# A quarter of the K and Q products of groups two to four computed as seven products of 2x2 blocks

## The chip, the cores and the metric

The kernel runs on one NeuronCore of one Trainium2 chip. TensorE multiplies matrices into PSUM; VectorE and ScalarE work on SBUF and PSUM; GpSimd does little here; SyncE issues nearly all DMA transfers. The engines run at the same time, each through its own queue in order, and wait for each other by semaphores. The metric is the device time of one execution, in microseconds.

## The reference

A decoder layer for 256 tokens of width 2048, in float32. Cut to what this change touches:

```python
h = rmsnorm(x, norm_mix_w[l])
proj = jnp.einsum('bsd,de->bse', h, w_in[l])
q, k, v, z, b_raw, a_raw, p_in, g_a, g_b = jnp.split(proj, splits, axis=-1)
qkv = jax.nn.silu(causal_dwconv(jnp.concatenate([q, k, v], axis=-1), conv_qkv_w[l]))
q, k, v = jnp.split(qkv, 3, axis=-1)
...
o = gated_delta_rule(q, k, v, g_log, beta).astype(x.dtype)
o = rmsnorm(o, gdn_norm_w[l]) * jax.nn.silu(z.reshape(bsz, seq, N_HEADS, HEAD_DIM))
...
mixed = jax.nn.sigmoid(g_a) * y_a + jax.nn.sigmoid(g_b) * y_b
x = x + jnp.einsum('bsd,de->bse', mixed, w_out[l])
```

Q, K, V, Z, the pooled input and the gates g_a and g_b are each 256 x 2048 products of the normalised tokens with a 2048 x 2048 part of `w_in`. The delta rule works in chunks of 64 tokens and solves a lower triangular system per chunk and head. Behind this come the output projection and a gated MLP with an up and a down projection.

## The kernel before

**Groups and weight tiles.** The 2048 output columns of each projection are cut into four groups of 512 (four heads each). A group computes K, Q, V, the pooled input, the gate GB, Z, a small pool product and the gate GA, in this order (the last group has the pool product and Z the other way round), and then the next group starts with K. Each projection of a group reads the 2048 features as eight weight tiles of 256 features (two feature blocks of 128) by 512 columns, 512 KB in float32. The names GA0 to GA7, K0 to K7 and so on below are these tiles.

**High and low parts.** TensorE multiplies in a float32 form of reduced precision, so each weight tile is cut in two: ScalarE casts `raw` to `whi` (L317), VectorE computes `wlo` = `raw` - `whi` (L328, "the split"). The tokens were cut the same way, into `xh` and `xl`. `gemm_a` multiplies per feature block and half of the tokens `whi` with `xh`, `whi` with `xl` and `wlo` with `xh` (L365 to L367): 12 matmuls of 512 columns a tile. The sums of a projection stand in a PSUM tile of pool `psm`, two banks, one per half of the tokens, and `psm` has two such tiles; `psg` has four of one bank.

**What sets the order.** The list `srcs` gives the weight tiles in their order of use. Whenever a product takes a tile from `weights`, tiles up to two further ahead are begun (`begin`: cast and split), and their loads (`load`) go into SyncE's queue; `raw` has four buffers, `whi` and `wlo` three. Between feature blocks `side()` advances a generator of side work, here the gated delta rule of the group (`gdn`); `later` holds functions that run when the next product has come to its second tile (`if c == 1`). The tile scheduler then orders each engine's queue by its own simulation of time; each engine works its queue strictly in order.

**The delta rule at a group's end.** While GA runs, the group's triangular systems are solved. VectorE does a forward substitution on small blocks (`tb`, L965 and L967). The result goes to DRAM and back (`tbd`, L972 and L975) and is transposed block by block on VectorE into `T` (L987). Then the inverse is put together from the blocks: TensorE L1011 (with L1018 beside it, from which VectorE makes `ro`, L1022), ScalarE copies into `U` (L1014), TensorE L1029, VectorE L1031 and L1032 (into `T` and `TT`), TensorE L1039, a ScalarE copy (L1041), TensorE L1047, VectorE L1048, and then the products with V and Q. At the same time the gate of Z stands in `sz`; after GA it is multiplied by GA's gate (ScalarE L1177, VectorE L1204) and by a norm weight (L1206).

**The up stage** of the MLP has for some of its column chunks another form already: the 2x2 blocks of a pair of weight chunks are loaded as four `quad` tiles, and seven products stand in for eight (the Winograd form of Strassen's scheme), named T1, 11, T2, 21, T3, 22 and T4. The products T1 to T4 take differences of blocks (`up_sum`, L244 on VectorE, in place), and T1, T2, T3 and 22 take sums of tokens. Between the products sums are copied or added in PSUM (ScalarE L1447 and L1451, VectorE L1433 and L1454). `high_first` issues one such product: six matmuls of 512 columns, the four with `whi` first.

Of the kernel before, what the change touches and what calls it, by code (L numbers as in the profile page):

```python
# [14 lines left out]
P = 128  # L15
S = 256
# [19 lines left out]
def kernel(  # L36
# [40 lines left out]
    def cols(w, base, nk):  # L77
        return [w[c * 256 : (c + 1) * 256, base : base + 512].rearrange("(k p) f -> p k f", p=P)
                for c in range(nk // 2)]

    srcs = []
    for g in range(4):
        for base in (C_K, C_Q, C_V, C_P, C_GB):
            srcs += cols(w_in[0], base + 512 * g, KD)
# [6 lines left out]
        srcs += cols(w_in[0], C_GA + 512 * g, KD)  # L91
# [6 lines left out]
    UP_PARTS = ("T1", "11", "T2", "21", "T3", "22", "T4")  # L98
    up_w = [(cols(w_up[0], 512 * c, KD), cols(w_up[0], DFF + 512 * c, KD)) for c in range(NUP)]
    up_steps = []  # L100
    TAIL = 3
    for c in range(NUP):
# [114 lines left out]
    def load_part(n, k):  # L217
        if n == len(loads):
            if isinstance(srcs[n], tuple):
# [9 lines left out]
    UP_HOMES = ((("xt0", "xt1", "xt2", "xt3"), ("hhi8", "hlo8", "hhi9", "hlo9")),  # L229
                (("xt0", "xt2", "xt1", "xt3"), ("hhi6", "hlo6", "hhi7", "hlo7")))  # L230

    def quad_load(c, n):

        ch, i = n // 4, (1, 0, 3, 2)[n % 4]
        up_quarters[c, ch, i] = fp.tile([P, 2, 512], F32, tag=UP_HOMES[1 - c % 2][ch][i], name=nm("quad"))
# [58 lines left out]
    def begin(n):  # L294
        while len(made) < min(len(srcs), n):
            load(len(made) + 1)
            raw = loads[len(made)]
            if isinstance(raw, tuple):
                raw, plus, minus = raw
                nc.vector.tensor_tensor(raw, plus, minus, op=ALU.subtract)  # L300
            src = srcs[len(made)]
            shape = list(raw.shape)
            keep = kept.get(len(made))
            behind_conv = ExitStack()
            for ins in last_conv.values():
# [11 lines left out]
            last_cast[0] = nc.scalar.copy(hi, raw).ins  # L317
            if shape[1] == 8:
                lo = None
                nc.vector.tensor_tensor(hi[:, :, 32:64], raw[:, :, 0:32], hi[:, :, 0:32].bitcast(F32),  # L320
                                        op=ALU.subtract)
            else:
                if fourth:
                    lo = fp.tile(shape, F32R, tag="s", name=nm("wlo"))
                else:
                    lo = wpool.tile(shape, F32R, tag="wlo", name=nm("wlo")) if keep is None else \
                        mtile(4 + keep, shape, F32R, nm("klo"))
                last_split[0] = nc.vector.tensor_tensor(lo, raw, hi.bitcast(F32), op=ALU.subtract).ins  # L328
# [22 lines left out]

    later = []

    def gemm_a(lh, ll, nk, steps=None, ps=None):

        ps = pm() if ps is None else ps
        for c in range(nk // 2) if steps is None else steps:
            if c == 1:
                while later:
                    later.pop(0)()  # L360
            hi, lo = weights()
            for kk in range(2):
                k = 2 * c + kk
                for t in range(2):
                    mm(ps[:, t, :], lh(k, t), hi[:, kk, :], start=(k == 0), stop=False)  # L365
                    mm(ps[:, t, :], ll(k, t), hi[:, kk, :], start=False, stop=False)  # L366
                    mm(ps[:, t, :], lh(k, t), lo[:, kk, :], start=False, stop=(k == nk - 1))  # L367
                side()
        return ps

    banks = [0]

# [487 lines left out]
    def gdn(g, kq, vt, conv, res):  # L860
# [231 lines left out]
        yield  # L1092
        res.append((po, ro))

    for g in range(4):
        kq = mp.tile([P, 4, 2, S], F32, tag="kq", bufs=1, name=nm("kq"))
        for kind, dst in ((1, kq[:, :, 0, :]), (0, kq[:, :, 1, :])):
            ps = ps_k0 if kind == 1 and g == 0 else gemm_a(xh, xl, KD)
            e = evict(ps)
            convs.append(conv_silu(e, kind, g, dst))  # L1100
            if g:
                later.append(lambda conv=convs[-1]: sum(1 for _ in conv))
            elif kind:

                later.append(lambda conv=convs[-1]: side_work.__setitem__(0, chain(conv, running_sums())))
            else:
                later.append(drain)
# [5 lines left out]
            0, along(gdn(g, kq, vt, v_conv(g, vt), res), conv)))  # L1113
        v_taps(g)
        if g == 0:
            def after_k(k_conv=k_conv[0]):
                with tc.issue_after(last_pow[0]), tc.issue_after(k_conv):
                    fixed_parts()
# [85 lines left out]
        nc.vector.scalar_tensor_tensor(sz, ta, 1.0, sz, op0=ALU.add, op1=ALU.mult)  # L1204
        sz4 = sz.rearrange("p t (h d) -> p (t h) d", h=4)
# [104 lines left out]
    def four_sums(a11, a12, a21, a22, hi, lo):  # L1310

        s = fp.tile([P, 4, S], F32, tag="s", name=nm("sums"))
        s1, s2, s3, s4 = (s[:, n].rearrange("p (k s) -> p k s", k=2) for n in range(4))
        nc.vector.tensor_tensor(s1, a21, a22, op=ALU.add)
        nc.vector.tensor_tensor(s2, s1, a11, op=ALU.subtract)
        nc.vector.tensor_tensor(s3, a11, a21, op=ALU.subtract)
        nc.vector.tensor_tensor(s4, a12, s2, op=ALU.subtract)
# [4 lines left out]
    def by_halves(h):  # L1322
        return [h[:, 2 * j : 2 * j + 2, t * P : (t + 1) * P] for t in range(2) for j in range(2)]

    y_d = {c: dpool.tile([P, 4, S], F32, tag=f"y{c}", bufs=1, name=f"y{c}") for c in (7, 8, 9)}

# [81 lines left out]

    def fl(k, t):
        return both(fhl, k)[:, 1, t * P : (t + 1) * P]  # L1410

    def high_first(uses, w, first=False):

        for n in range(2):
            for kk in range(2):
                for ps, high, low in uses:
                    for lhs in (high, low) if n == 0 else (high,):
                        mm(ps, lhs(kk), w[n][:, kk], start=(first and n == 0 and kk == 0 and lhs is high), stop=False,  # L1418
                           skip_group_check=True)

    def up_product(c, what, ch):

# [315 lines left out]
```

## Time and profile before

| what | value |
| --- | --- |
| runs | 1537.75, 1536.89, 1536.61 us; median 1536.89 |
| profiled execution: span | 1536.8 us (the page gives no time of its own beside it) |
| instructions | 20233 |
| ScalarE busy | 853.1 us (56%) |
| GpSimd busy | 80.9 us (5%) |
| HBM traffic | 203 GB/s over the span |
| end of the last chain | PE 30% of the span, all others below 1% |

The profile is that of one execution. A row of a group of instructions has the line of the kernel, the engine, the operation, the output and inputs by their tile names, the count, and behind the bar the busy time and the mean in ns of one, then the idle time of the engine just before these instructions with what ended most of it. A row of the timeline starts with the time in us from the span's start and the duration; a number in brackets is the time for which the engine stood idle before it, with the engine, tile and line that ended the wait. A row of waits names the waiting group, the one that releases it, then the total in us, the number of waits and the longest. A row of one tile has the durations in ns (least, median, most) and the first and last start. A row of windows has the stretch, then its length, the busy us of TensorE, its weight load, VectorE, ScalarE and GpSimd, the granted TensorE clock, the DMA share and GB/s. Matmuls overlap: each lasts some 0.39 us, but they follow each other at a shorter spacing.

### The profile page before, as it was taken

What the parts mean: (1) busy time and instruction counts of PE and PEld (TensorE: products, weight loads), DVE (VectorE), ACT (ScalarE), POOL (GpSimd) and SP (SyncE); (2) the same over time, 40 slices, a digit from 0 to 9 for tenths busy, and PEclk for the clock granted to TensorE, in tenths of its full rate; (3) what the DMA queues carried; (4) which work ended last, traced back from release to release, by engine and by line L of the source; (5) the groups of instructions that cost most, each with busy time, mean ns of one, the idle gap of its engine ahead of it and who ended that gap; (6) DMA issues with size and microseconds to landing.
All of it is one profiled execution on the core that took longest, in us unless ns stands there. A gap on an engine that the chain in (4) does not pass through costs nothing. (4 is left out here: it accounts for less than half of the span.)

```text
span 1536.8 us, 20233 instructions
## 1 busy us (share of the span) xinstructions
PE 1524.3 (99%) x7290; PEld 1255.4 (82%) x7290; DVE 1268.3 (83%) x1793; ACT 853.1 (56%) x1070; POOL 80.9 (5%) x105
## 2 busy tenths in 40 slices
PE   9999999999999999999999999999999999999997
PEld 8887888787878888788888888788888888888876
DVE  6788859896589858887567899999999886889896
ACT  6455446454455445454455666666666665555553
POOL 1010002000100000000000000000000011010200
PEclk9999999999999999999999999999999999999999
DMA  8776757776576766776588556656457478566662
GB/s 276 209 229 198 203 165 207 218 216 185 148 250 201 208 169 194 231 195 186 171 263 305 179 178 219 219 206 206 154 165 243 127 238 266 172 223 207 235 201 98
DMA packets 166515, 313.62 MB, mean 204 GB/s; under 512 B 19554, under 2 KB 23426, under 8 KB 166286
## 3 DMA queue, kind: packets, MB, share of 16 engines
q1 hardware_dynamic: 157280, 283.17, 59.2%
q0 software_dynamic: 7344, 27.27, 5.5%
q10 hardware_dynamic: 1790, 1.89, 0.4%
q8 instruction: 57, 0.93, 0.3%
q14 instruction: 44, 0.36, 0.1%
HBM read 303.33 MB, written 8.95 MB: 203 GB/s over the span
## 5 line engine op out<-in xcount | busy, mean ns | idle before, releaser
L317 ACT CAST whi<-raw 128x1024 fp32r<-128x1024 f32 x420 | 441.2, 1052 | 427.1 <-PE psm L366 270.0
L328 DVE TENSOR_TENSOR wlo<-raw,whi 128x1024 fp32r<-128x1024 f32 x418 | 507.7, 1220 | 146.0 <-ACT whi L317 140.2
L317 ACT CAST whi<-quad 128x1024 fp32r<-128x1024 f32 x182 | 190.5, 1053 | 136.8 <-PE psg L1418 43.5
L328 DVE TENSOR_TENSOR wlo<-quad,whi 128x1024 fp32r<-128x1024 f32 x182 | 220.0, 1219 | 30.0 <-ACT whi L317 29.4
L367 PE MATMUL psm<-wlo,xhl 128*128 128x512 f32 x432 | 169.5, 393 | 1.3 <-DVE wlo L328 1.2
L365 PE MATMUL psm<-whi,xhl 128*128 128x512 f32 x432 | 169.0, 391 | 0.0
L366 PE MATMUL psm<-whi,xhl 128*128 128x512 f32 x432 | 168.6, 390 | 0.0
L1418 PE MATMUL psg<-whi,fhl 128*128 128x512 f32 x504 | 127.2, 390 | 0.0
L1418 PEld LDWEIGHTS psg<-whi,fhl 128*128 128x128 f32 x504 | 94.5, 188 | 19.6
L367 PEld LDWEIGHTS psm<-wlo,xhl 128*128 128x128 f32 x432 | 81.1, 188 | 18.8 <-DVE wlo L328 2.2
L366 PEld LDWEIGHTS psm<-whi,xhl 128*128 128x128 f32 x432 | 81.1, 188 | 16.8
L365 PEld LDWEIGHTS psm<-whi,xhl 128*128 128x128 f32 x432 | 81.1, 188 | 16.7
L244 DVE TENSOR_TENSOR quad<-quad,quad 128x1024 f32<-128x1024 f32 x72 | 87.6, 1216 | 0.0
L1418 PE MATMUL psg<-wlo,fhl 128*128 128x512 f32 x252 | 69.9, 389 | 0.0
L1418 PE MATMUL psg<-whi,ups 128*128 128x512 f32 x216 | 58.9, 394 | 0.0
L1418 PEld LDWEIGHTS psg<-wlo,fhl 128*128 128x128 f32 x252 | 47.3, 188 | 9.9
L1403 PE MATMUL psm<-whi,hhi 128*128 128x512 f32 (+1 forms) x140 | 54.5, 389 | 0.1
L1403 PE MATMUL psm<-whi,hlo 128*128 128x512 f32 (+1 forms) x140 | 54.1, 386 | 0.0
L1403 PE MATMUL psm<-wlo,hhi 128*128 128x512 f32 (+1 forms) x140 | 54.0, 387 | 0.0
L365 PE MATMUL psm<-whi,mhi 128*128 128x512 f32 x128 | 50.8, 397 | 0.0
L367 PE MATMUL psm<-wlo,mhi 128*128 128x512 f32 x128 | 50.0, 390 | 0.0
L366 PE MATMUL psm<-whi,mlo 128*128 128x512 f32 x128 | 49.9, 390 | 0.0
(435 smaller groups left out, 2953.7 us busy)
## 6 DMA issues: line engine op xcount, KB each, us to landing
raw<-in_w_in_dram SPq DMA_DIRECT2D x224, 512.0 KB, 4.3
raw<-in_w_up_dram SPq DMA_DIRECT2D x104, 512.0 KB, 4.8
quad<-in_w_up_dram SPq DMA_DIRECT2D x72, 512.0 KB, 5.0
raw<-in_w_down_dram SPq DMA_DIRECT2D x56, 512.0 KB, 5.1
raw<-in_w_out_dram SPq DMA_DIRECT2D x32, 512.0 KB, 4.2
quad<-in_w_down_dram POOLq DMA_DIRECT2D x32, 512.0 KB, 5.3
mv<-vrow SPq DMA_DIRECT2D x12, 512.0 KB, 4.8
taps<-in_conv_qkv_w_dram SPq DMA_DIRECT2D x16, 256.0 KB, 6.6
```

The source lines that it names most:

```text
L244: nc.vector.tensor_tensor(out_, plus_, minus_, op=ALU.subtract)
L317: last_cast[0] = nc.scalar.copy(hi, raw).ins
L328: last_split[0] = nc.vector.tensor_tensor(lo, raw, hi.bitcast(F32), op=ALU.subtract).ins
L365: mm(ps[:, t, :], lh(k, t), hi[:, kk, :], start=(k == 0), stop=False)
L366: mm(ps[:, t, :], ll(k, t), hi[:, kk, :], start=False, stop=False)
L367: mm(ps[:, t, :], lh(k, t), lo[:, kk, :], start=False, stop=(k == nk - 1))
L1403: mm(ps[:, cs], lhs(kk), part_[:, kk, cs], start=(first and kk == 0 and n == 0), stop=(last and kk == 1 and n == 2), skip_group_check=shared)
L1418: mm(ps, lhs(kk), w[n][:, kk], start=(first and n == 0 and kk == 0 and lhs is high), stop=False, skip_group_check=True)
```

## The change

For groups two to four the first four feature blocks (tiles 0 and 1) of K and of Q are no longer computed as four weight tiles of 12 matmuls. The tokens' halves and the feature halves of these four blocks make 2x2 blocks, and K's and Q's columns with the feature halves make 2x2 blocks of weights; seven products of six matmuls give both projections' sums over these features.

- **Order.** The previous group's GA tiles are followed by the first two products: GA5, 11, GA6, T1, GA7 (`KQ_FIRST`). The next K opens with T2, 21, T3, then K2, then 22, K3, T4 and K4 to K7 (`KQ_THEN`). Q starts at its third tile.
- **PSUM.** `pair_product` works on two `psm` tiles: `a` (later K's sums) and `b` (Q's). After T1, ScalarE copies `a[0]` into `own` in SBUF and `a[1]` into `a[0]`. Before 21, VectorE adds `b[0]` = `a[1]` + `own`; after T3, `b[1]` = `a[1]` + `own`.
- **Weights.** The four blocks are loaded by SyncE into buffers of other tiles that are free then (`KQ_HOMES`), one each from six tiles ahead of product 11 on (`quads_behind`); their differences are made by `up_sum` in place, on VectorE, ahead of the cast of each product (`sums_behind`).
- **Tokens.** The sums of the tokens are made once, in group one (`x_sums`), from the high and low parts, and kept cut in high and low in two tiles. `sums_into` is code that the MLP had already.
- **Later work.** For K and Q of groups two to four `later` is run at the fourth tile and not at the second (`flush=3`).

```diff
+    KQ_FIRST = (5, "11", 6, "T1", 7)
+    KQ_THEN = ("T2", "21", "T3", 2, "22", 3, "T4", 4, 5, 6, 7)
...
+            if g and base == C_K:
+                srcs += [("up", ("kq", g), step, 0) if isinstance(step, str) else tiles[step] for step in KQ_THEN]
+            else:
+                srcs += tiles[2:] if g and base == C_Q else tiles
...
+        srcs += tiles[: 5 if g < 3 else 8]
+        if g < 3:
+            srcs += [("up", ("kq", g + 1), step, 0) if isinstance(step, str) else tiles[step] for step in KQ_FIRST]
...
+    quads_behind = {}
+    for g in range(1, 4):
+        sums_behind[first_part(("kq", g)) - 1] = [(("kq", g), "T1", 0)]
+        for i in range(4):
+            quads_behind[first_part(("kq", g), "11") - 6 + i] = [(("kq", g), i)]
...
+    KQ_HOMES = ("crow", "mv", "pu", "pa")
...
+            home = mp.tile([P, 2, 512], F32, tag=KQ_HOMES[i], name=nm("quad"))
...
+            for more in quads_behind.get(len(made) - 1, ()):
+                quad_load(*more)
...
+    def pair_product(bank, what, tokens, sums):
+
+        a, b = bank["ps"]
+        if what in ("11", "21", "T4"):
+            j, t = {"11": (0, 0), "21": (1, 0), "T4": (1, 1)}[what]
+            high, low = (lambda kk, f=f: f(2 * j + kk, t) for f in tokens)
+        else:
+            n = {"T1": 0, "T2": 1, "T3": 2, "22": 3}[what]
+            high, low = (lambda kk, s=s: s[:, n, kk * P : (kk + 1) * P] for s in sums)
+        if what == "21":
+            nc.vector.tensor_tensor(b[:, 0], a[:, 1], bank["own"], op=ALU.add)
+        w = weights()
+        ps = {"T1": a[:, 0], "21": a[:, 0], "22": b and b[:, 0]}.get(what, a[:, 1])
+        high_first([(ps, high, low)], w, what in ("T1", "11"))
+        if what == "T1":
+            bank["own"] = cpool.tile([P, 512], F32, tag="sqj", name=nm("own"))
+            nc.scalar.copy(bank["own"], a[:, 0])
+            nc.scalar.copy(a[:, 0], a[:, 1])
+        elif what == "T3":
+            nc.vector.tensor_tensor(b[:, 1], a[:, 1], bank["own"], op=ALU.add)
...
+    def x_sums():
+
+        h = mp.tile([P, 4, S], F32, tag="mv", name=nm("whole"))
+        for j in range(2):
+            nc.vector.tensor_tensor(h[:, 2 * j : 2 * j + 2], xhl[j][:, :, 0, :].bitcast(F32),
+                                    xhl[j][:, :, 1, :].bitcast(F32), op=ALU.add)
+        s = mp.tile([P, 4, S], F32, tag="pu", name=nm("sums"))
+        sums_into(s, *by_halves(h))
+        hi, lo = (mtile(i, [P, 4, S], F32R, nm("xs")) for i in (3, 7))
+        nc.scalar.copy(hi, s)
+        nc.vector.tensor_tensor(lo, s, hi.bitcast(F32), op=ALU.subtract)
+        xsums.extend((hi, lo))
...
-            ps = ps_k0 if kind == 1 and g == 0 else gemm_a(xh, xl, KD)
+            if g == 0:
+                ps = ps_k0 if kind else gemm_a(xh, xl, KD)
+            elif kind:
+                pair_bank["ps"] = ps, b = pair_bank["ps"][0], pm()
+                kq_steps(KQ_THEN, ps)
+            else:
+                ps = gemm_a(xh, xl, KD, range(2, 8), pair_bank["ps"][1], 3)
...
-            ps = gemm_a(xh, xl, KD)
+            ps = gemm_a(xh, xl, KD, range(5))
+            pair_bank["ps"] = pm(), None
+            kq_steps(KQ_FIRST, ps, 1)
```

**Where the instructions stand, VectorE before.** This is VectorE's queue at the end of group one, from the last step of the forward substitution on. The splits (`wlo`) behind it are those of K0, K1, K2, K3 and K4.

```order
L967 TENSOR_TENSOR tb_1345<-tb_1345,tmp_1346 128x8
L328 TENSOR_TENSOR wlo_1889<-raw_1885,whi_1887 128x1024
L328 TENSOR_TENSOR wlo_1907<-raw_1903,whi_1905 128x1024
L987 STREAM_TRANSPOSE T<-TT 32x8x32 x4
L328 TENSOR_TENSOR wlo_1944<-raw_1940,whi_1942 128x1024
L1204 SCALAR_TENSOR_TENSOR sz_1592<-gate_1921,sz_1592 128x1024
L328 TENSOR_TENSOR wlo_1976<-raw_1972,whi_1974 128x1024
L1206 TENSOR_TENSOR sz_1592<-sz_1592,gwb 128x1024
L1022 TENSOR_SCALAR ro_1646<-psg_1644 32x8 x4
L328 TENSOR_TENSOR wlo_1994<-raw_1990,whi_1992 128x1024
```

Four splits and the two multiplications of `sz` stand between the substitution and L1022, and the four transposes stand together.

**VectorE in the changed kernel, same place.** Lines have moved: L967 is L1021, L328 is L349, L987 is L1041, L1022 is L1076, L1204 is L1303, the block sums are L265. The splits here are those of T1, GA7, T2 and 21; the sums are those of T2, T3 and T4.

```order
L1021 TENSOR_TENSOR tb_1357<-tb_1357,tmp_1358 128x8
L349 TENSOR_TENSOR wlo_1907<-quad_1616,whi_1905 128x1024
L349 TENSOR_TENSOR wlo_1920<-raw_1916,whi_1918 128x1024
L265 TENSOR_TENSOR quad_1616<-quad_1733,quad_1616 128x1024
L1041 STREAM_TRANSPOSE T<-TT 32x8x32 x3
L349 TENSOR_TENSOR wlo_1936<-quad_1616,whi_1934 128x1024
L265 TENSOR_TENSOR quad_1671<-quad_1616,quad_1671 128x1024
L1041 STREAM_TRANSPOSE T<-TT 32x8x32
L349 TENSOR_TENSOR wlo_1951<-quad_1773,whi_1949 128x1024
L1076 TENSOR_SCALAR ro_1660<-psg_1658 32x8 x4
L1303 SCALAR_TENSOR_TENSOR sz_1604<-gate_1965,sz_1604 128x1024
L265 TENSOR_TENSOR quad_1616<-quad_1773,quad_1616 128x1024
```

Three block sums stand now in this stretch, and the last transpose stands behind T2's split and T3's sum. VectorE's queue goes on with the first add (L405), T3's split, the inverse's L1085 and L1086 (L1031 and L1032 before), K2's and 22's splits and the second add (L414):

```order
L405 TENSOR_TENSOR psm_1983<-psm_1885,own_1946 128x512
L349 TENSOR_TENSOR wlo_1986<-quad_1671,whi_1984 128x1024
L1085 TENSOR_SCALAR T<-psg_1679 32x2x2x32 x2
L1085 TENSOR_SCALAR T<-psg_1692 32x2x2x32 x2
L349 TENSOR_TENSOR wlo_1999<-raw_1995,whi_1997 128x1024
L1305 TENSOR_TENSOR sz_1604<-sz_1604,gwb 128x1024
L1086 STREAM_TRANSPOSE TT<-T 32x2x2x32 x4
L349 TENSOR_TENSOR wlo_2009<-quad_1733,whi_2007 128x1024
L414 TENSOR_TENSOR psm_1983<-psm_1885,own_1946 128x512
```

Both adds read `psm_1885`, the two-bank tile `a`, and write `psm_1983`, which is `b`; they stand in one queue with the inverse's operations.

**TensorE at the same place.** Before, behind the inverse's first piece (L1011), the last matmuls of K1 and the first of K2 stand there; a row ends with the engines whose semaphores it waits for, ScalarE (Activation) for the cast and VectorE (DVE) for the split:

```order
L365 MATMUL psm_1939<-whi_1905,xhl_114 128x512
L366 MATMUL psm_1939<-whi_1905,xhl_114 128x512
L367 MATMUL psm_1939<-wlo_1907,xhl_114 128x512
L365 MATMUL psm_1939<-whi_1942,xhl1a 128x512 [waits Activation_49]
L366 MATMUL psm_1939<-whi_1942,xhl1a 128x512
L367 MATMUL psm_1939<-wlo_1944,xhl1a 128x512 [waits DVE_49]
```

In the changed kernel, behind the inverse's second piece, the products 21 and T3 stand there (L422 is `high_first`), then L1093, L1101 (L1039 and L1047 before) and K2 (L389):

```order
L422 MATMUL psm_1885<-whi_1949,xhl_114 128x512 [waits DVE_49]
L422 MATMUL psm_1885<-whi_1949,xhl_114 128x512 x3
L422 MATMUL psm_1885<-wlo_1951,xhl_114 128x512 x2
L422 MATMUL psm_1885<-whi_1984,xs_772 128x512 [waits Activation_49]
L422 MATMUL psm_1885<-whi_1984,xs_773 128x512
L422 MATMUL psm_1885<-whi_1984,xs_772 128x512
L422 MATMUL psm_1885<-whi_1984,xs_773 128x512
L422 MATMUL psm_1885<-wlo_1986,xs_772 128x512 [waits DVE_49]
L422 MATMUL psm_1885<-wlo_1986,xs_772 128x512
L1093 MATMUL psg_1711<-T,ga_122_817 64x64 [waits DVE_49]
```

Product 21 writes `a[0]`, the bank beside the one that the first add reads; its first matmul waits for VectorE up to that add, and K2's first matmul (L389, behind the inverse's pieces) waits for VectorE up to the second add.

More of the change, by code (lines that the diff above doesn't have):

```diff
@@ L79, in cols @@
                 for c in range(nk // 2)]
+    UP_PARTS = ("T1", "11", "T2", "21", "T3", "22", "T4")
+    KQ_FIRST = (5, "11", 6, "T1", 7)
+    KQ_THEN = ("T2", "21", "T3", 2, "22", 3, "T4", 4, 5, 6, 7)
+    up_w = {("kq", g): [cols(w_in[0], base + 512 * g, KD) for base in (C_K, C_Q)] for g in range(1, 4)}
     srcs = []
@@ L97 @@
     chunks_of = [()] + [(1, 0) if c in TWO else (0,) for c in range(1, NUP)]
-    UP_PARTS = ("T1", "11", "T2", "21", "T3", "22", "T4")
-    up_w = [(cols(w_up[0], 512 * c, KD), cols(w_up[0], DFF + 512 * c, KD)) for c in range(NUP)]
+    up_w |= {c: (cols(w_up[0], 512 * c, KD), cols(w_up[0], DFF + 512 * c, KD)) for c in range(NUP)}
     up_steps = []
@@ L364, in gemm_a, with high_first @@
                 for t in range(2):
-                    mm(ps[:, t, :], lh(k, t), hi[:, kk, :], start=(k == 0), stop=False)
-                    mm(ps[:, t, :], ll(k, t), hi[:, kk, :], start=False, stop=False)
-                    mm(ps[:, t, :], lh(k, t), lo[:, kk, :], start=False, stop=(k == nk - 1))
+                    mm(ps[:, t, :], lh(k, t), hi[:, kk, :], start=(k == 0), stop=False, **seeded)
+                    mm(ps[:, t, :], ll(k, t), hi[:, kk, :], start=False, stop=False, **seeded)
+                    mm(ps[:, t, :], lh(k, t), lo[:, kk, :], start=False, stop=(k == nk - 1), **seeded)
                 side()
         return ps
+    def pair_product(bank, what, tokens, sums):
[17 more added lines that the diff above has]
+            nc.vector.tensor_tensor(b[:, 1], a[:, 1], bank["own"], op=ALU.add)
+    def high_first(uses, w, first=False):
+        for n in range(2):
+            for kk in range(2):
+                for ps, high, low in uses:
+                    for lhs in (high, low) if n == 0 else (high,):
+                        mm(ps, lhs(kk), w[n][:, kk], start=(first and n == 0 and kk == 0 and lhs is high), stop=False,
+                           skip_group_check=True)
     banks = [0]
@@ L1093, in gdn, with by_halves, sums_into, kq_steps @@
         res.append((po, ro))
+    def by_halves(h):
+        return [h[:, 2 * j : 2 * j + 2, t * P : (t + 1) * P] for t in range(2) for j in range(2)]
+    def sums_into(s, a11, a12, a21, a22):
+        s1, s2, s3, s4 = (s[:, n].rearrange("p (k s) -> p k s", k=2) for n in range(4))
+        nc.vector.tensor_tensor(s1, a21, a22, op=ALU.add)
+        nc.vector.tensor_tensor(s2, s1, a11, op=ALU.subtract)
+        nc.vector.tensor_tensor(s3, a11, a21, op=ALU.subtract)
+        nc.vector.tensor_tensor(s4, a12, s2, op=ALU.subtract)
+    xsums = []
+    def x_sums():
[9 more added lines that the diff above has]
+        xsums.extend((hi, lo))
+    pair_bank = {}
+    def kq_steps(steps, ps, flush=3):
+        for step in steps:
+            if isinstance(step, str):
+                pair_product(pair_bank, step, (xh, xl), xsums)
+            else:
+                gemm_a(xh, xl, KD, (step,), ps, flush)
     for g in range(4):
@@ L1115 @@
         if g == 0:
+            later.append(x_sums)
             def after_k(k_conv=k_conv[0]):
@@ L1312, in four_sums @@
         s = fp.tile([P, 4, S], F32, tag="s", name=nm("sums"))
[L1313 to L1317, printed above, removed]
+        sums_into(s, a11, a12, a21, a22)
         nc.scalar.copy(hi, s)
@@ L1410, in fl @@
         return both(fhl, k)[:, 1, t * P : (t + 1) * P]
[L1412 to L1419, printed above, removed]
     def up_product(c, what, ch):
```

16 lines of the change are left out of this document (9 added, 7 removed).

## The prediction

> **What bounds the kernel now.** I read the spans and the busy times first, then TensorE's waits, then the engines' timelines at the three places that the edit touches.
>
> ```profile
> core 0: 1536.8 us, clock 0.998
> ```
> ```profile
> PE 1524.3 (99%) x7290; PEld 1255.4 (82%) x7290; DVE 1268.3 (83%) x1793; ACT 853.1 (56%) x1070; POOL 80.9 (5%) x105
> ```
> ```profile
> PE psm L367 <- DVE wlo L328: 1.5, 2, 1.2
> PE psg L1418 <- DVE wlo L328: 1.2, 3, 0.8
> ```
>
> TensorE is busy 99% of the span, and the longest of its waits is 1.2 us. So a matmul that is removed is worth its spacing, and a microsecond for which TensorE is made to wait is lost in full. VectorE (83%) has room on average; what counts is its room at those three places.
>
> I call them boundary 1, 2 and 3: the end of GA of group one, two, three with K of the next. GA5 is GA's sixth weight tile, K2 is K's third. Time zero of a boundary is GA5's start on TensorE. At boundary 1 these are GA5's first matmul and GA6's, then (the view of one tile, with the first and last start of each group) the four pieces of the finished group's triangular inverse:
>
> ```profile
> 175.84 0.39 PE L365 MATMUL psm<-whi,xhl2b 128*128 128x512 f32 x1
> ...
> 178.56 0.39 PE L365 MATMUL psm<-whi,xhl 128*128 128x512 f32 x1
> ```
> ```profile
> L1011 PE MATMUL psg<-T,ga x32: 191/191/212, 188.8 to 189.9; 32*32 32x32 f32 x32
> L1029 PE MATMUL psg<-U,TT x32: 191/191/212, 194.6 to 195.1; 32*32 32x32 f32 x32
> L1039 PE MATMUL psg<-T,ga x16: 218/218/267, 200.9 to 201.8; 64*64 64x64 f32 x16
> L1047 PE MATMUL psg<-TT,U x16: 218/218/267, 206.7 to 207.6; 64*64 64x64 f32 x16
> ```
>
> Twelve matmuls take 2.72 us, 0.2267 each. First to last start plus one duration makes the inverse's pieces 1.3, 0.7, 1.1 and 1.1 us, together 4.2.
>
> VectorE at the same place: a weight tile's split, the last step of the forward substitution, the block transposes behind it, and three costs that I need:
>
> ```profile
> 176.90 1.23 DVE L328 TENSOR_TENSOR wlo<-raw,whi 128x1024 fp32r<-128x1024 f32 x1 [0.26 <-ACT whi L317]
> ...
> 178.66 0.18 DVE L967 TENSOR_TENSOR tb<-tb,tmp 128x8 f32<-128x8 f32 x1
> ...
> 185.82 1.84 DVE L987 STREAM_TRANSPOSE T<-TT 32x256 f32<-32x256 f32 x4 [2.25 <-DMA TT<-tbd]
> ...
> 188.83 1.22 DVE L1204 SCALAR_TENSOR_TENSOR sz<-gate,sz 128x1024 f32<-128x1024 f32 x1
> 189.97 1.22 DVE L328 TENSOR_TENSOR wlo<-raw,whi 128x1024 fp32r<-128x1024 f32 x1
> ...
> 192.24 0.68 DVE L1022 TENSOR_SCALAR ro<-psg 32x8 f32<-32x8 f32 x4
> ```
> ```profile
> L1031 DVE TENSOR_SCALAR T<-psg x4: 284/290/297, 195.9 to 196.9; 32x128 f32<-32x128 f32 x4
> L1032 DVE STREAM_TRANSPOSE TT<-T x4: 300/304/307, 197.2 to 198.2; 32x128 f32<-32x128 f32 x4
> ```
>
> A 128x1024 operation in a full queue costs 1.14 (188.83 to 189.97); L1031's and L1032's fours cost 1.3 each. A split comes 1.06 after the tile two places ahead of it starts on TensorE (176.90 against 175.84). From the substitution's end (178.84) to the transposes lie 6.98 us of DMA through DRAM. VectorE stands 2.25 of them in front of the transposes, and TensorE does not feel it: two finished tiles of 2.72 us lie ahead of it.
>
> **The change part by part.** The gain: per group, four tiles of 12 matmuls become seven of 6, so 42 for 48; three groups make 18 x 0.2267 = **4.1 us**.
>
> The additions, per group: three more casts and splits, four block sums, two adds out of PSUM, two ScalarE copies. The prices of the last two stand in the up stage, which has the same operations; beside them ScalarE's rows at boundary 1 (cast, gate, U copies):
>
> ```profile
> L1433 DVE TENSOR_TENSOR psg<-psg,own 128x512 f32<-128x512 f32 x10 | 6.9, 690 | 0.0
> ```
> ```profile
> L1451 ACT COPY psg<-psg 128x512 f32<-128x512 f32 x10 | 5.8, 583 | 0.0
> ```
> ```profile
> 183.97 1.05 ACT L317 CAST whi<-raw 128x1024 fp32r<-128x1024 f32 x1 [1.67 <-PE psm L366]
> 184.92 1.26 ACT L1177 ACTIVATE gate<-psm,rsh 128x512 f32<-128x512 f32 x2
> ...
> 189.89 1.10 ACT L1014 COPY U<-psg 32x128 f32<-32x128 f32 x4 [2.15 <-PE psg L1011]
> ```
>
> VectorE gets 7 x 1.14 + 2 x 0.69 = 9.4 us more at each boundary, where a product of six matmuls feeds TensorE for 1.36 us and costs VectorE 2.28 when it needs a block sum. The order's waits add the point that decides: product 21 does not start before the first add (L405), and K2 not before the second (L414). Between them and the transposes stand, in VectorE's queue, the inverse's own operations. So K2 starts when that queue has reached L414. Without waits TensorE would come to K2 after three GA tiles (8.2), five products (6.8) and the inverse (4.2): **19.2**.
>
> Boundary 1. GA6's split starts at 1.06, the T1 sum follows it and pushes the substitution's end from 3.0 to 4.1; its blocks land 6.98 later, at 11.1. VectorE has by then done two splits and the T2 sum (8.0) and stands 3.1 us in front of the transposes, with the splits of T2, 21 and T3 behind them. From 11.1: three transposes 1.4, T2's split, the T3 sum 2.3, the fourth transpose 0.5, 21's split 1.1, ro 0.7, sz and the T4 sum 2.3, the first add 0.7: 20.1, and only then 21. TensorE is ready for it at about 15.2 (transposes 12.5, two pieces of the inverse 1.4, T2 1.4). On: T3's split 1.1, L1085 (once L1031) 1.3, K2's split and sz 2.3, L1086 (once L1032) 1.3, 22's split 1.1, the second add 0.7: **27.9**. Lost: 27.9 - 19.2 = 8.7.
>
> At boundaries 2 and 3 the order puts the substitution's last five and last two steps right behind 11's split, which ends at -0.5 (one tile ahead of GA6's); at some 0.22 a step it ends at 0.6 and 0.0. The last step and the transposes of before:
>
> ```profile
> 355.93 0.18 DVE L967 TENSOR_TENSOR tb<-tb,tmp 128x8 f32<-128x8 f32 x1
> ...
> 362.82 1.84 DVE L987 STREAM_TRANSPOSE T<-TT 32x256 f32<-32x256 f32 x4 [1.78 <-DMA TT<-tbd]
> ...
> 535.43 0.18 DVE L967 TENSOR_TENSOR tb<-tb,tmp 128x8 f32<-128x8 f32 x1
> ...
> 541.63 1.37 DVE L987 STREAM_TRANSPOSE T<-TT 32x256 f32<-32x256 f32 x3 [1.75 <-DMA TT<-tbd]
> ```
>
> The round trips are 6.7 and 6.0, so blocks land at 7.3 and 6.0. Boundary 2 from 7.3 to L414: eleven operations of 1.14, transposes 1.9, ro 0.7, L1085 and L1086 2.6, two adds 1.4: 19.1, so K2 at **26.4**, lost 7.2. Boundary 3: T2's cast stands behind the U copies and both new copies on ScalarE: T1 ends at 8.8, own copy 0.6, U 1.1 (from 9.7), the other copy 0.6, cast 1.05: 12.5. From there nine operations of 1.14, L1085, L1086 and two adds: 14.3, so **26.8**, lost 7.6 (one more small piece of the inverse stands there on both engines; left out).
>
> Sum: 8.7 + 7.2 + 7.6 - 4.1 = **+19.4**. On the profiled execution's 1536.8, which is the runs' median (1536.89) to 0.1, that is **1556**.
>
> At nothing I cost two things. The token sums, once in group one: six short operations of at most 0.69 and a split, at most 5.3 us of VectorE, which stands idle for 3 of 10 us there; without cover, +5.3 at most. And the blocks' loads: the same bytes, asked for a few tiles earlier, where a tile takes 4.3 us to land and its buffer comes free some 8 us before its cast.
>
> ```profile
> 30.00:40.00 10.00, 10.00 (x47) 7.94 (x47) 6.97 (x13) 6.43 (x9) 3.32 (x6) 1.00 0.90 288
> ```
> ```profile
> raw<-in_w_in_dram SPq DMA_DIRECT2D x224, 512.0 KB, 4.3
> ```
>
> **The rivals.** *Not slower: VectorE keeps up.* If at each boundary L414 is done by 19.2, only the gain is left: 1532.7. For it: the up stage streams the same seven products with VectorE at 96% (238.95 of 250 us) and hardly a wait.
>
> ```profile
> 900.00:1150.00 250.00, 248.66 (x1141) 205.57 (x1140) 238.95 (x249) 168.89 (x197) 0.00 (x0) 1.00 0.55 181
> ```
>
> Against it: from 1.06 on the queue to L414 holds 14 operations of 1.14 and 6.5 us of others (boundary 1 0.8 more), 22.5 us of work for 18.1 of time.
>
> *The queue alone.* If VectorE never stands idle in that queue, L414 is done at 24.4, 23.5 and 23.5: 13.8 lost, +9.7, **1546.5**. That is the least that the order allows.
>
> *The clock falls with the waits.* 21 comes after some 5 us without a matmul at boundary 1. Were the granted clock (1.00 in every row above) to halve from there through 21 and T3, twelve matmuls would take 0.2267 more each: 2.7 a boundary, 8.2 in all, **1564**. [...]
>
> *No change.* The waits would have to be 4.1 in all, 1.4 a boundary; nothing points there: 1536.9.
>
> **How the numbers follow.** The walk (1556) 0.72; the queue alone (1546.5) 0.10; the clock (1564) 0.08; VectorE keeps up (1532.7) 0.07; no change 0.03. The forecast's own uncertainty is the round trip and the casts, about 2 us a boundary: 1550 to 1562. Taking in the queue alone and the clock, the range is **1546 to 1565**. 0.2% (3.1 us) is about what a measurement can tell from no change. Faster 0.07, within 0.03, slower 0.90.
>
> **What would show it.** In the changed profile: TensorE's waits for VectorE in front of 21 (L405) and of K2 (L414), each of several us, three times; VectorE idle some 3 us for DMA at boundary 1's transposes and then full until L414; the stretch from GA5 to K2 near 27 us instead of 19; 18 matmuls of 512 columns fewer; the clock still 1.0. Wrong I would be if TensorE's waits sum to under 13 us, or if they lie elsewhere, at weight tiles or DMA.

## The result, and the profile after

The changed kernel took 1559.67 us (median of 4 runs, 1558.4 to 1563.24) against 1536.78 us before: 22.9 us longer, a ratio of 1.0149 with a 95% interval of 1.0137 to 1.0162. The forecast was 1556 with a range of 1546 to 1565. The profiled execution has a span of 1558.0 us, 21.2 more than that of before.

The view of the cores and the page's busy times of the changed kernel:

```profile
core 0: 1558.0 us, clock 0.991
...
PE 1530.9 (98%) x7272; PEld 1258.8 (81%) x7272; DVE 1300.4 (83%) x1827; ACT 866.3 (56%) x1086; POOL 77.0 (5%) x105
```

The 18 matmuls are gone (7272 for 7290), and VectorE has 32 us more. The mean granted clock has fallen from 0.998 to 0.991, which the forecast had not. The waits of TensorE (waiting group, releaser, total us, times, longest):

```profile
PE psm L422 <- DVE psm L405: 7.8, 3, 3.1
PE psm L391 <- DVE wlo L349: 2.3, 4, 1.1
PE psg L1101 <- issue: 2.2, 1, 2.2
PE psm L389 <- DVE psm L414: 1.4, 2, 1.3
PE psg L1108 <- DVE TT L1102: 1.0, 1, 1.0
```

The two adds stand there as releasers, in front of 21 (L422) and of K2 (L389). Together these five are only 14.7 us. To see the rest one has to go to the timeline. TensorE at boundary 1 of the changed kernel: GA5, product 11, the inverse's second piece, 21, the last of T3, K2.

```profile
175.71 0.39 PE L389 MATMUL psm<-whi,xhl2b 128*128 128x512 f32 x1
...
178.43 1.07 PE L422 MATMUL psm<-whi,xhl 128*128 128x512 f32 x4
...
190.19 0.69 PE L1083 MATMUL psg<-U,TT 32*32 32x32 f32 x32
194.02 2.08 PE L422 MATMUL psm<-whi,xhl 128*128 128x512 f32 x4 [3.14 <-DVE psm L405]
...
198.45 1.06 PE L422 MATMUL psm<-wlo,xs 128*128 128x512 f32 x2
...
202.15 0.50 PE L389 MATMUL psm<-whi,xhl1a 128*128 128x512 f32 x1 [0.16 <-DVE psm L414]
```

K2 starts 26.4 us after GA5. The four matmuls of 21 last 2.08 where those of product 11 last 1.07: they run at half speed. The granted clock in windows of 2 us (window, its length, busy us of TensorE, weight load, VectorE, ScalarE and GpSimd, then the clock, DMA share, GB/s):

```profile
192.00:194.00 2.00, 0.00 (x0) 0.00 (x0) 1.97 (x4) 0.00 (x0) 0.00 (x0) 0.81 0.00 0
194.00:196.00 2.00, 1.98 (x5) 1.61 (x6) 1.91 (x4) 0.00 (x0) 0.00 (x0) 0.50 0.00 0
...
200.00:202.00 2.00, 1.99 (x30) 1.72 (x28) 1.94 (x3) 0.73 (x2) 0.00 (x0) 0.98 0.34 131
...
386.00:388.00 2.00, 2.00 (x6) 1.54 (x5) 0.77 (x3) 0.00 (x0) 0.00 (x0) 0.50 0.34 52
```

In the first three of these windows VectorE is busy for 1.9 us out of 2 or more; TensorE waits in the first and runs at half speed in the second, and by the third the clock is back. The fourth lies behind K2 of boundary 2. VectorE's queue at boundary 1 (the substitution's last step, the transposes, the two adds):

```profile
179.68 0.18 DVE L1021 TENSOR_TENSOR tb<-tb,tmp 128x8 f32<-128x8 f32 x1
...
184.76 1.37 DVE L1041 STREAM_TRANSPOSE T<-TT 32x256 f32<-32x256 f32 x3 [0.93 <-DMA TT<-tbd]
...
193.26 0.70 DVE L405 TENSOR_TENSOR psm<-psm,own 128x512 f32<-128x512 f32 x1
...
201.39 0.70 DVE L414 TENSOR_TENSOR psm<-psm,own 128x512 f32<-128x512 f32 x1
```

From the transposes to L414 it never waits. K2 follows the end of L414 (202.09) by 0.06. GA5 and K2 at boundaries 2 and 3, and the piece of the inverse ahead of K2 at boundary 3:

```profile
358.77 0.39 PE L389 MATMUL psm<-whi,xhl2b 128*128 128x512 f32 x1
...
385.05 0.80 PE L389 MATMUL psm<-whi,xhl1a 128*128 128x512 f32 x1 [1.25 <-DVE psm L414]
...
544.76 0.39 PE L389 MATMUL psm<-whi,xhl2b 128*128 128x512 f32 x1
...
571.58 1.61 PE L1108 MATMUL psg<-vt,TT 128*128 128x128 f32 x8 [1.02 <-DVE TT L1102]
572.85 0.77 PE L389 MATMUL psm<-whi,xhl1a 128*128 128x512 f32 x1
```

And K2 in the kernel before, at the same three places:

```profile
190.84 0.39 PE L365 MATMUL psm<-whi,xhl1a 128*128 128x512 f32 x1
...
368.32 0.40 PE L365 MATMUL psm<-whi,xhl1a 128*128 128x512 f32 x1
...
547.16 0.39 PE L365 MATMUL psm<-whi,xhl1a 128*128 128x512 f32 x1
```

From GA5 to K2 it was 15.0 us at each boundary; now it is 26.4, 26.3 and 28.1, in all 35.8 more. From K2 to the next GA5, or to the end, it was 162.5, 163.8 and 989.6, and is 156.6, 159.7 and 985.2: 14.5 less, since products and pieces of the inverse that stood there now stand ahead of K2. 35.8 - 14.5 = 21.3, the whole difference.

### The profile page after: what moved, and what is told of

It is laid out like the page before. It is cut to its first block, busy times and chain, and to the rows that moved or that the text cites. A ratio compares the mean times of both kernels' runs of the same rounds, so it can differ in the third digit from the quotient of the medians.

```text
span 1558.0 us, 20231 instructions
## 1 busy us (share of the span) xinstructions
PE 1530.9 (98%) x7272; PEld 1258.8 (81%) x7272; DVE 1300.4 (83%) x1827; ACT 866.3 (56%) x1086; POOL 77.0 (5%) x105
## 5 line engine op out<-in xcount | busy, mean ns | idle before, releaser
L338 ACT CAST whi<-raw 128x1024 fp32r<-128x1024 f32 x408 | 428.3, 1052 | 396.4 <-PE psm L390 250.5
L349 DVE TENSOR_TENSOR wlo<-raw,whi 128x1024 fp32r<-128x1024 f32 x406 | 494.4, 1223 | 129.0 <-ACT whi L338 124.5
L338 ACT CAST whi<-quad 128x1024 fp32r<-128x1024 f32 x203 | 212.0, 1052 | 178.4 <-PE psg L422 45.9
L349 DVE TENSOR_TENSOR wlo<-quad,whi 128x1024 fp32r<-128x1024 f32 x203 | 246.4, 1224 | 45.5 <-ACT whi L338 44.5
L391 PE MATMUL psm<-wlo,xhl 128*128 128x512 f32 x384 | 150.2, 392 | 2.0 <-DVE wlo L349 2.0
L389 PE MATMUL psm<-whi,xhl 128*128 128x512 f32 x384 | 150.2, 391 | 0.0
L390 PE MATMUL psm<-whi,xhl 128*128 128x512 f32 x384 | 149.5, 389 | 0.0
L422 PE MATMUL psg<-whi,fhl 128*128 128x512 f32 x504 | 127.2, 389 | 0.0
L422 PEld LDWEIGHTS psg<-whi,fhl 128*128 128x128 f32 x504 | 94.5, 188 | 19.6
L265 DVE TENSOR_TENSOR quad<-quad,quad 128x1024 f32<-128x1024 f32 x84 | 102.6, 1222 | 0.1
L391 PEld LDWEIGHTS psm<-wlo,xhl 128*128 128x128 f32 x384 | 72.1, 188 | 18.2 <-DVE wlo L349 3.2
L390 PEld LDWEIGHTS psm<-whi,xhl 128*128 128x128 f32 x384 | 72.1, 188 | 14.8
L389 PEld LDWEIGHTS psm<-whi,xhl 128*128 128x128 f32 x384 | 72.1, 188 | 14.6
L422 PE MATMUL psg<-wlo,fhl 128*128 128x512 f32 x252 | 69.9, 390 | 0.0
L422 PE MATMUL psg<-whi,ups 128*128 128x512 f32 x216 | 58.8, 394 | 0.0
L422 PEld LDWEIGHTS psg<-wlo,fhl 128*128 128x128 f32 x252 | 47.3, 188 | 9.8
L389 PE MATMUL psm<-whi,mhi 128*128 128x512 f32 x128 | 50.8, 397 | 0.0
```

The costliest lines, as they stand in the source:

```text
L265: nc.vector.tensor_tensor(out_, plus_, minus_, op=ALU.subtract)
```

## The experiments

The theory going in: VectorE's queue is full between the transposes and the second add; 21 and K2 wait for adds in that queue; so time is lost in VectorE operations. The rivals: the halved clock is the main cost; or TensorE's own chain (the inverse, the casts) sets K2. Lines of an experiment's own kernel differ by a few from those above; `high_first` is L422 to L438 in them. To measure K2 without GA5's row I take product 11's first matmul to K2's: in the changed kernel 23.7, 23.6 and 25.4 us.

**Without the block sums.** The kernel leaves out the sums, so its products are not those of the layer; only its time is of use.

```diff
     def up_sum(c, what, ch):
+        if isinstance(c, tuple):
+            return
```

> Left out: the block sums of the K and Q products (twelve VectorE operations); the products read the plain blocks. The queue (VectorE's work up to the second add sets K2): at each boundary three sums of 1.14 us stand between the transposes' data and the second add, so K2 comes 3.4 us sooner, 10.3 us in all; the wait before 21 falls under 1 us, the clock stays at 1.0, and the 4.2 us that K2 and what follows lose at half clock are saved too: 1545. The clock alone: the falls go, 1547 to 1550. Neither (TensorE's own chain, the inverse or the casts, sets K2): within 3 us of 1559.7.

Measured: 1551.26 us, before on the same chip 1537.58 (ratio 1.0089, 1.0074 to 1.0104). Product 11 and K2 at boundaries 2 and 3:

```profile
360.97 1.07 PE L424 MATMUL psm<-whi,xhl 128*128 128x512 f32 x4
...
380.76 0.56 PE L391 MATMUL psm<-whi,xhl1a 128*128 128x512 f32 x1 [1.25 <-DVE psm L416]
...
542.62 1.07 PE L424 MATMUL psm<-whi,xhl 128*128 128x512 f32 x4
...
562.42 0.79 PE L391 MATMUL psm<-whi,xhl1a 128*128 128x512 f32 x1 [1.25 <-DVE psm L416]
```

19.8 us at both, and 21.3 at boundary 1: K2 comes 2.4, 3.8 and 5.6 sooner, 11.7 in all, where the queue said 3.4 each and 10.3 in all; at boundary 3 the slow matmuls ahead of K2 go with the sums. The rival that had K2 set by TensorE's own chain said no gain, and is out; but the casts, which wait for the sums, come sooner here too, and the next run leaves them alone. The wait before 21 fell from 7.8 to 4.1 us (2.4 of them at boundary 1) and not under 1. The clock did not stay up: it fell at each boundary, for 3.4 us each time, and waits for splits of plain tiles grew from 2.3 to 5.7. So some 9 us were saved (22.9 and 13.7 over before, each against its own runs) and not 15.

**The multiplications of sz behind the second add.**

```diff
-            gated()
+            def behind(sized=sized, gated=gated):
+                with tc.issue_after(pair_bank["add"]):
+                    sized()
+                gated()
+            later.append(behind)
```

(`sized` holds the two operations; `pair_bank["add"]` is the second add. `gated`, which needs their result, is put off with them.)

> The two multiplications of sz (1.14 us each on VectorE) are put behind the second add. The queue: the second add and K2 come 2.3 us sooner at each boundary, 6.9 in all: 1553, and down to 1549 if the clock then stays up. TensorE's own chain sets K2: within 3 us of 1559.7.

Measured: 1550.71 us (1.0084, 1.0067 to 1.01). Product 11 to K2: 21.7, 21.3 and 23.3 us, so 2.0, 2.3 and 2.0 sooner. Two operations of 1.14 us that nobody waits for at this place, moved a few rows down a queue, are worth 6.3 us at K2 and some 9.8 in all (22.9 and 13.1 over before). What the putting off of `gated` adds to the second figure was not measured by itself. The granted clock's low stretch at boundary 1 shrank from 6.8 to 3.4 us.

**More matmuls in the gaps.**

```diff
         if what == "21":
+            for _ in range(10):
+                mm(b[:, 1], xh(0, 0), bank["w"][0][:, 0], start=True, stop=True, skip_group_check=True)
...
         elif what == "T3":
+            for _ in range(8):
+                mm(b[:, 1], xh(0, 0), w[0][:, 0], start=True, stop=True, skip_group_check=True)
```

> Added: ten matmuls that nobody reads between T2 and 21, eight between T3 and K2, at each boundary, so that TensorE has no long gap there. The queue: K2 starts where it did, 26 to 28 us after GA5, since VectorE's queue is the same; only the slow matmuls behind K2 at the second and third boundary (4.2 us) are saved: 1555. The clock as the main cost: 21, T3 and K2 run at full speed at all three boundaries and K2 starts sooner: 1547 to 1550. Added matmuls in the way: above 1560.

Measured: 1570.56 us (1.0217, 1.0202 to 1.0232). It settles nothing about the clock: the added matmuls were scheduled ahead of T2 at two boundaries, so that everything behind T2 came later, and the gap that they were to fill grew; the wait before 21 went from 7.8 to 11.0 us, longest 4.8, and the clock fell for 6.8 us at each boundary. What it shows is only that matmuls put in TensorE's queue without a tie to the gap did not land in the gap.

**A gap by itself, in the kernel before.** With n of 4 and of 10:

```diff
+                    ps = gemm_a(xh, xl, KD, range(4), skip_group_check=True)
+                    for _ in range(n):
+                        nc.scalar.copy(ps[:, 0], ps[:, 0])
+                    ps = gemm_a(xh, xl, KD, range(4, 8), ps, skip_group_check=True)
```

> The kernel before, with one wait put into Z of each of groups one to three, far from the group's end: between Z3 and Z4 ScalarE copies a bank of Z's PSUM tile onto itself four times (0.58 us each), and Z4 has to wait for it. No clock fall with a gap this short: three gaps of 2.3 to 2.8 us, 1544 to 1546. If any gap lets the clock fall: 1550 or more.

> The same with ten copies: gaps of 5.8 to 6.3 us, 17.4 to 18.9 in all. If a gap costs only itself: 1555 to 1557. If the clock halves in the gap and stays there for the 6.4 to 6.8 us that the changed kernel showed at its three boundaries, up to 3.3 us more each where the gap does not hide it: 1560 to 1566.

Measured: 1559.16 us with four copies, 1570.33 with ten, before 1537.73. The three gaps of the kernel with four, and its clock around the second and third:

```profile
152.88 0.79 PE L365 MATMUL psm<-whi,xhl2a 128*128 128x512 f32 x1 [5.59 <-ACT psm L1195]
...
337.48 0.50 PE L365 MATMUL psm<-whi,xhl2a 128*128 128x512 f32 x1 [3.24 <-ACT psm L1195]
...
519.64 0.80 PE L365 MATMUL psm<-whi,xhl2a 128*128 128x512 f32 x1 [3.24 <-ACT psm L1195]
```
```profile
338.00:341.00 3.00, 3.00 (x8) 2.32 (x8) 2.70 (x9) 0.00 (x0) 0.00 (x0) 0.51 0.53 159
341.00:344.00 3.00, 3.00 (x14) 2.45 (x13) 2.19 (x5) 1.05 (x1) 0.00 (x0) 0.92 0.00 0
```
```profile
518.00:520.00 2.00, 0.36 (x1) 0.36 (x2) 1.86 (x6) 1.53 (x3) 0.00 (x0) 0.74 0.90 249
520.00:522.00 2.00, 2.00 (x6) 1.52 (x6) 1.81 (x6) 0.00 (x0) 0.00 (x0) 0.50 0.65 189
```

(The pairs of windows are 3 us and 2 us long.) The gaps were longer than the copies (2.38 us), because casts stood ahead of them in ScalarE's queue. All three let the clock fall, the ones of 3.24 too. Read in windows of a quarter of a microsecond, the clock is at half for 6.8, 3.4 and 6.8 us; with ten copies (22.8 us of gaps) for 10.2, 6.8 and 6.8. After the gap TensorE is busy for 4.2, 3.4 and 6.0 of them, and half of that is lost: 6.8 us. With four copies 12.1 of gaps, 6.8 of clock and 2.3 more of waits for splits make 21.2 of the 21.4 measured; with ten, 22.8, 6.5 and 3.1 make 32.4 of 32.6. These terms are read from the profiled executions, whose spans are 21.7 and 30.8 us longer than that of before, so the sums are good to 0.5 and 1.6 us. A gap of this size (3.24 to 5.59 us) cost itself and, by half of the 3.4 to 6.0 us busy at half clock, an estimated 1.7 to 3 us more. What I had expected of the short gap was wrong.

**The add's operand taken out of PSUM by ScalarE.** One edit that takes the waits for the adds from 21 and K2 and leaves VectorE's work in place:

```diff
-            nc.vector.tensor_tensor(b[:, 0], a[:, 1], bank["own"], op=ALU.add)
+            bank["sum"] = mp.tile([P, 2, 512], F32, tag="cy", bufs=2, name=nm("sum"))
+            nc.scalar.copy(bank["sum"][:, 0], a[:, 1])
+            nc.vector.tensor_tensor(b[:, 0], bank["sum"][:, 0], bank["own"], op=ALU.add)
```

(and the same for the second add)

> The changed kernel with one edit: before 21 and after T3 ScalarE copies a[1] into SBUF, and VectorE adds from there, so 21 and K2 wait for ScalarE (0.58 us) and no longer for the adds; VectorE's operations and their order stay nearly the same. The queue: the waits in front of 21 and K2 go, but 22 writes into b and still waits for the second add, in the same queue, about one plain tile later; some 2.5 us a boundary are saved and the wait stands in front of 22: 1549 to 1554. If the wait of 21 and K2 for the adds is all there is: 1535 to 1540. If TensorE's inverse or the casts set the time: within 3 us of 1559.7.

Measured: 1553.43 us (1.0106, 1.0091 to 1.0121). K2 of boundary 1 now starts 20.8 us after GA5, 5.6 sooner, as its waits allow; then TensorE waits for the next thing that VectorE owes:

```profile
202.39 0.65 PE L1104 MATMUL psg<-TT,U 64*64 64x64 f32 x8 [0.81 <-DVE TT L1089]
203.56 0.50 PE L391 MATMUL psm<-wlo,xhl1b 128*128 128x512 f32 x1 [0.52 <-DVE wlo L349]
```

The time is the one expected and the place is not: at boundary 1 it is not 22 behind the second add that waits, but the inverse (L1104, which was L1101) and a product that needs the split of K3. At boundaries 2 and 3 the clock still falls for 6.8 us each, with TensorE busy for 12 of these in all, so by half of that some 6 of the 15.4 us over before are slow matmuls. Freed of one wait, TensorE runs into the same full queue a few operations on.

**The products later, in a tile of their own.** Both the place and the way of adding are changed: K2 and K3 come first, and the products 11, T1, T2 and T3 go into `b` while K's plain tiles go into `a`, so that no plain tile of K waits for an add.

```diff
+    KQ_STEPS = (("K", 2), ("K", 3), "11", ("K", 4), "T1", ("K", 5), "T2", ("K", 6), "T3", ("K", 7), "21", ("Q", 2), "22",
+                ("Q", 3), "T4")
...
+        ps = {"11": b[:, 1], "T1": b[:, 0], "T2": b[:, 1], "T3": b[:, 1], "21": a[:, 0], "22": b[:, 0], "T4": a[:, 1]}[what]
...
+        elif what == "T2":
+            nc.vector.tensor_tensor(b[:, 0], b[:, 1], bank["T1"], op=ALU.add)
...
+            nc.vector.tensor_tensor(b[:, 1], b[:, 1], bank["T1"], op=ALU.add)
+        elif what == "T4":
+            nc.vector.tensor_tensor(a[:, 0], a[:, 0], bank["11"], op=ALU.add)
+            nc.vector.tensor_tensor(a[:, 1], a[:, 1], bank["T3"], op=ALU.add)
```

> The same seven products, moved: K2 and K3 first, then the products between K4 to K7, Q2 and Q3, where VectorE was less than half busy before (200 to 230 us). K's plain sums are in their own PSUM tile, so no plain tile waits for an add; the price is four adds and three copies a group for two and two. If the place is the cause (a full VectorE queue at the group's end), most of the gain of 4.1 us is kept: 1533 to 1538. If seven products cost VectorE too much wherever they stand: 1545 to 1560.

Measured: **1533.26 us** (7 runs), before 1537.58: ratio 0.9969, 0.9958 to 0.9980. It beats both kernels. The windows of 10 us behind boundary 1, of the kernel before and then of this one:

```profile
200.00:210.00 10.00, 10.00 (x67) 7.97 (x66) 4.33 (x5) 3.73 (x5) 0.00 (x0) 1.00 0.56 160
210.00:220.00 10.00, 10.00 (x55) 8.57 (x54) 3.75 (x4) 4.91 (x6) 0.00 (x0) 1.00 0.54 157
```
```profile
200.00:210.00 10.00, 10.00 (x68) 8.04 (x68) 9.61 (x11) 5.02 (x7) 0.00 (x0) 1.00 0.28 67
210.00:220.00 10.00, 10.00 (x56) 8.57 (x55) 6.62 (x10) 5.83 (x9) 0.00 (x0) 1.00 0.48 144
```

The same additions (and two adds and a copy more) fill what was empty on VectorE, 4.33 of 10 before and 9.61 now, and TensorE is busy all the time. The clock is 1.00 in both. The gain is 4.3 us (3.1 to 6.5 by the interval); the matmuls alone said 4.1.

Two things differ here from the changed kernel, place and way of adding. Two more runs part them.

**The same, earlier.** Only the order's line differs from the last kernel; product 11 follows GA7 and not K3, which is two tiles, 5.4 us (the expectation says 8):

```diff
+    KQ_STEPS = ("11", ("K", 2), "T1", ("K", 3), "T2", ("K", 4), "T3", ("K", 5), "21", ("K", 6), "22", ("K", 7), "T4")
```

> The moved version (products in their own PSUM tile, no plain tile behind an add) with one line changed: product 11 ahead of K2 and one product behind each of K2 to K7, some 8 us earlier, beside the inverse. If the place decides (VectorE's queue is full there): TensorE waits for splits of T2, K4 and T3, 3 to 4 us a boundary, 1540 to 1546. If it was the plain tiles' wait for the adds that decided, and not the place: 1533 to 1536, as with the later place.

Measured: 1539.36 us (10 runs), before 1537.73 (1.0014, 1.0004 to 1.0024). TensorE's first wait:

```profile
PE psm L391 <- DVE wlo L349: 5.0, 6, 1.5
```

The time lies between the two ranges expected. The waits are for splits, as the place would have it, but fewer.

**The same, at the changed kernel's place.**

```diff
+    KQ_FIRST = (("G", 5), "11", ("G", 6), "T1", ("G", 7))
+    KQ_STEPS = ("T2", ("K", 2), "T3", "21", ("K", 3), "22", ("K", 4), "T4", ("K", 5), ("K", 6), ("K", 7))
```

("G" tiles are those of GA.)

> The moved version's way of adding (products in b, K's plain tiles in a, four adds and three copies), with the products at the changed kernel's place: 11 and T1 between GA5 to GA7, then T2, K2, T3, 21, K3, 22, K4, T4. Queue and waits together: VectorE is as full as there, but plain tiles fill part of the time for which T3 and 22 wait for adds; some 3 us lost a boundary, 1540 to 1544. The place alone decides: 1550 or more. The waits of plain tiles for adds alone decide: 1533 to 1536.

Measured: 1548.99 us, before 1538.03 (1.0072, 1.0055 to 1.0089), between the two values expected.

```profile
PE psm L394 <- DVE wlo L352: 6.2, 8, 1.6
```

Each against its own runs of before: the changed kernel +22.9; the other way of adding at the same place +11.0; 5.4 us later (product 11 behind GA7 and not behind GA5) +1.6; another 5.4 later -4.3. So the place is worth 15.3 us, and the way of adding, with the mixing of products and plain tiles that it allows, 11.9 (the mixing differs a little among the last three, too). By the intervals each of these two is good to about 3 us. The 11.9 holds for the early place alone: the first way of adding was not run at the later place. In this last series the clock falls at no boundary (1.00 in every window there), so the 11.9 takes in the slow matmuls that the changed kernel had behind K2.

## Why the prediction was right, and where it was not

**The time and the sign** were right, by the mechanism named: VectorE's queue up to L414 sets K2's start. L405 stands as the releaser of 21 at all three boundaries (3.1, 1.8 and 2.9 us). L414 stands as that of K2 at two, for 0.2 and 1.3 us, where the forecast had several us three times: slow matmuls and pieces of the inverse filled part of that time, and at boundary 3 the last release is that of L1108 by L1102, the row ahead of L414 in the same queue. The two operations of `sz` taken out of that queue brought K2 forward by about their own length at each boundary; the sums did so in all, though not boundary by boundary.

**The gain** of 4.1 could not be seen in the changed kernel; the later place shows 4.3.

**The walks.** GA5 to K2 was forecast at 27.9, 26.4 and 26.8, and measured at 26.4, 26.3 and 28.1: lost 7.2, 7.1 and 8.9, together 23.2 for 23.5. That the sum is this close is partly luck. At boundary 1 the mis-sized term was the round trip through DRAM: 6.98 us in the profile of before, 4.9 here (179.86, the end of the substitution, to 184.76), so VectorE stood 0.93 and not 3.1 us in front of the transposes. (TensorE's readiness for 21 at 15.2 counts 1.4 for two pieces of the inverse that its own rows give as 1.3 and 0.7; the sum does not use it.) At boundary 3 it was the small piece of the inverse that I left out: L1102 stands in front of L414 and L1108 in front of K2, which is about the missing 1.3. The two terms put at nothing were nothing: GA5 of boundary 1 starts at 175.71 for 175.84 before, with the token sums (34 to 42 us) behind it, and no wait of TensorE was ended by a DMA.

**The step that failed** is "the clock still 1.0". It fell at all three boundaries, for 6.8, 6.8 and 6.8 + 3.4 us. The rival that had this event had it at the wrong place and so at the wrong price. It charged 21 and T3 with 2.7 us a boundary, 8.2 in all; but at boundary 1, 21 and T3 did run at half speed and lost 3.0 us, and K2 then waited 0.16 us for L414. The queue hid the slow matmuls. What counts is the half clock behind K2, where nothing hides it: about 3.1 us at boundary 2 and 1.3 at boundary 3 (half of TensorE's busy time from K2 to the clock's return, 6.2 and 2.7 us), 4.4 together. This is read from the trace; that a fall cost half of the busy time under it is what the two gap kernels showed by their sums (21.2 of 21.4 us, 32.4 of 32.6), and the spacing of K2's matmuls at boundary 2 (0.43 us for 0.23) agrees. The attempt to take it away in the changed kernel itself miscarried.

That the clock would halve, and just for 21 and T3, was my assumption in that rival: its rows of before have 1.00, and no run shows its 2.7 us as the price of a boundary. The runs showed a clock of 0.50 (194 to 196 and 386 to 388 us of the changed kernel) with 0, 3.1 and 1.3 us lost behind K2 at the three boundaries. How long a wait must be for a fall no run shows; two gaps of 3.24 us had one.

**The sum as it came out:** 23.2 + 4.4 - 4.1 = 23.5, against 21.2 in the profiled executions and 22.9 in the medians. Of what is over, L1108's 1.3 us at boundary 3 are counted in the 23.2 and missing behind K2; where the rest went stays open.

**The rivals.** "VectorE keeps up" (1532.7) is what happens at the later place, to within a microsecond: the argument for it, the up stage, was sound, and what it lacked was room on VectorE at this place. "The queue alone" (1546.5) fell, though VectorE waited less than I had it wait. The threshold that I gave for being wrong (TensorE's waits under 13 us) was a poor one: of the 28 us lost some 10 are slow matmuls (3.0 and 2.2 ahead of K2, 4.4 behind it), which no list of waits shows.

## What to carry to other kernels

A cheaper product is worth its matmuls only where the engine that prepares it has room at that place; the mean over the span (83% here) tells nothing about it, and 10-us windows do. When an accumulation must be read by another engine midway, give it a tile that the next plain work doesn't use, and put plain work between: of 27 us between the worst and the best version of the same arithmetic, 12 went with this at the early place and 15 with the place. And after a wait of some 3 us on TensorE (here 3.14 and 3.24, each with a clock of 0.50 behind it), look at the granted clock before adding up waits.

## What the runs showed that I had not expected

The clock's falls came in pieces: every one that I measured, in seven kernels, lasted 3.4, 6.8 or 10.2 us. The windows of a quarter of a microsecond give each turn to a few hundredths: the share of the window at half clock tells where it lies. A fall and a return of the changed kernel:

```profile
193.00:193.25 0.25, 0.00 (x0) 0.00 (x0) 0.23 (x1) 0.00 (x0) 0.00 (x0) 0.97 0.00 0
200.00:200.25 0.25, 0.25 (x7) 0.25 (x6) 0.22 (x2) 0.00 (x0) 0.00 (x0) 0.87 1.10 426
```

Read so, its turns, down and up, stand at 193.24, 200.06, 384.38, 391.21, 561.88, 568.71, 572.12 and 575.53 us. They lie 0, 2, 56, 58, 108, 110, 111 and 112 steps of 3.413 us behind the first, to 0.01 us, over the whole stretch of 382 us; the turns of the six other kernels fit the same step, each from its own first turn. So every turn that I read lies at a multiple of one step behind its kernel's first turn, and the falls had no fixed distance from TensorE's last work: they began 0.3 to 4.5 us after the last matmul of 512 columns or, three times, when TensorE was already back at work, as in the second gap of the kernel with four copies (338.07, 0.6 us after). What sets a turn no run here shows. At boundary 2 of the changed kernel the clock fell at 384.38, some 4 us after T3's end (380.2), with 1.4 us of the inverse's 64x64 matmuls between.
